# Refill instructions tied behind left operands, weight sums moved, two accumulating transfers issued later

## Chip, cores and metric

The kernel runs on one core of a Trainium2 chip. The metric is the device time of one execution in microseconds (us).

## What is computed

One layer of a bidirectional encoder with two branches, in float32, for 1024 positions, 16 meta tokens ahead of them and 1024 channels:

```python
u = rms_norm(h, pre_w)
rq, rk, rv, rg, aq, ak, av, ag, gr, ga = split(u @ w_in)
# branch A: retention, 4 heads, forward and backward scans in chunks of 128
o_r = group_norm(retention(rotary(rq), rotary(rk) * 128**-0.5, rv)) * ret_nw * silu(rg)
y_r = o_r @ w_rb
# branch B: softmax attention in a window of +-128 keys, 8 heads, meta keys, a sink logit
o_a = attention(rotary(aq), rotary(ak), av, sink) * silu(ag)
y_a = o_a @ w_ab
mix = sigmoid(gr) * y_r + sigmoid(ga) * y_a
out = h + rms_norm(mix @ w_o, post_w)
```

## The kernel before

Every large product is made three times on TensorE: an operand is split into a high part, which is its value rounded to a shorter float, and a low part, which is what the rounding left, and `mm3` multiplies high by high, low by high and high by low. So each operand costs a cast (mostly on ScalarE, `nc.scalar.copy`, sometimes on GpSimd, `pool_hi`) and a subtraction on VectorE (`dve_lo`, line 92). In the text this subtraction is "the lower part".

The work runs in this order. First come projections of the queries and keys, the retention of four heads, then attention. While attention's blocks run, projections that come later are put between them as filler. Then there are four phases of large products: z (the gate projections, 16 units), r (w_rb), a (w_ab) and o (w_out). In these four phases a product of 2x2 blocks is done with seven block products instead of eight, from sums and differences of the blocks. PROD lists the seven with their left and right operands: B11, T1, B21, T2, T3, B22 and T4 are the right operands, kept in SBUF for the whole phase, each as four pieces k = 0 to 3 in a high and a low part. They lie in the tile `big` (B11, T1, B21, B22, and T4's last piece in its margins) and in tiles named T (T2, T3, T4). A left operand belongs to one unit and one product: `prepare` builds it, from a weight tile (`wr..`) or from a sum (`st..S`), up to LEAD = 6 products ahead, and `split` makes its high part (`lh`) and its low part (`ll`); six buffers each.

`run` walks through all products in order. At each step it prepares left operands up to six products ahead, issues the product of twelve matmuls, and then calls what the dictionary `hooks` holds for this index. Two kinds of work hang there:

- The refill of the right operands for the next phase (`refill`, called for z, r and a; it is named after the phase that it runs in, so the tiles of the refill in z are named z). It loads blocks, forms differences (`minus`, line 1157), and splits them into the right operands as soon as the running phase is done with each. Indices are counted from the end of the phase: -17 is 17 products before it, 4 is after the fifth product of the next phase. The refill of phase a is another one, which gets most right operands ready-made from DRAM.
- The sums of the output weights for phase o, in four groups k = 0 to 3: `pre_load` fetches four blocks (SP), and four calls of `pre_split` each form one difference on VectorE (line 776), its high part (ScalarE) and its low part (VectorE), and write both to DRAM (SP). They are tied behind the latest sum out of PSUM (`near`).

The order in which each engine executes its instructions is not the program's. A planner simulates the kernel when it is built, with costs of its own, and fills each engine's queue with what is ready, the earlier in the program first; a later instruction can thus be put ahead of an earlier one that is not ready in the simulation. On the chip an engine works through its queue in order. `tc.issue_after(ins)` adds only an order: what is traced inside comes behind `ins` in the queue of `ins`'s engine, and instructions of other engines are not bound.

In attention, `stage1` of a block makes the scores, the exponentials, a reciprocal (`den`, line 1438) and the scaling of two weight tiles on GpSimd (line 1447), followed by two small copies on GpSimd (`pool_hi`, line 89). `stage2` transposes the scaled weights on TensorE (lines 1463 to 1468). `rope_late` turns queries and keys by their position: two products on VectorE, and two transfers issued on GpSimd that add the turned halves in place (line 187). Names of its tiles are like aq3_10: head pair 3, half 1, head 0 of the pair. `split_q` (line 669) later casts the turned queries.

Of the kernel before, what the change touches and what calls it, by code (L numbers as in the profile page):

```python
# [10 lines left out]
ALU = mybir.AluOpType  # L11
# [28 lines left out]
def block_kernel(ctx: ExitStack, tc: tile.TileContext, x0, xT, x, meta, w_in, w_rb, w_ab, w_out, post_w,  # L40
                 rope, tab, out):
    nc = tc.nc
# [48 lines left out]
    def dve_lo(o, i, hi):  # L91
        return nc.vector.tensor_tensor(o, i, hi.bitcast(F32), ALU.subtract).ins  # L92
# [84 lines left out]
    cr = ra.tile([P, T], F32, name="cr")  # L177
    sr = ra.tile([P, T], F32, name="sr")

    def rope_late(t, a, b, o, nm):  # L180

        n = b - a
        m = ra.tile([P, 512], F32, tag="m", bufs=4, name=f"m_{nm}")
        nc.vector.tensor_tensor(m[:, 0:n], t[:, 0:n], sr[:, a:b], ALU.mult)
        nc.vector.tensor_tensor(o[:, 0:n], t[:, 0:n], cr[:, a:b], ALU.mult)
        for r in (0, 64):
            nc.gpsimd.dma_start(o[64 - r:128 - r, 0:n], m[r:r + 64, 0:n], accum_op=ALU.add)

    def rope_evac(t, a, b, o, nm):
        n = b - a  # L190
# [75 lines left out]
    with tc.tile_pool(name="setup", bufs=1, reuse_waits="tile") as st:  # L266
# [87 lines left out]
        split, wv0 = halves_w(U_V)  # L354
# [409 lines left out]
    def pre_load(k, src):  # L764

        w[k] = {}
        for i, j in ((0, 0), (0, 1), (1, 1), (1, 0)):
            w[k][i, j] = t = stage(f"w{i}{j}{k}", 1)
            src(t, 4 * i + k, j)
# [12 lines left out]
        if n == "T4":  # L782
            del w[k]

    w, near = {}, []
    gates = [U_G + u for u in range(4)] + [U_AG + u for u in range(4)] + [U_GR + u for u in range(8)]

    def pre_fetch(u):
# [71 lines left out]
    softmax, last = [], {}  # L860
# [96 lines left out]
    class Phase:  # L957
# [18 lines left out]
        def split(self, u, p, src):  # L976
            h, l = (lp.tile([P, 4, P], R, tag=t, bufs=LEAD, name=f"{t}{self.nm}{u}_{p}") for t in ("lh", "ll"))
            nc.scalar.copy(h, src)
            dve_lo(l, src, h)
            self.ops[u, p] = h, l  # L980

        def prepare(self, u, p):
# [162 lines left out]
    def refill(nm, src):  # L1145

        x = {}

        def load(i, j, ks=range(4)):
            def f():  # L1150
                for k in ks:
                    x[i, j, k] = t = stage(f"{nm}{i}{j}{k}", j)
                    src(t, 4 * i + k, j)
            return f

        def minus(o, a, b):
            return lambda k: nc.vector.tensor_tensor(x[*o, k], x[*a, k], x[*b, k], sub)

        def split(n, i, j):
            return lambda k: split_b(n, k, x[i, j, k])  # L1160

        def each(at, n, *fs):
            for k in range(4):
                at.setdefault(n + k if len(fs) > 1 else n + k // 2, []).extend([lambda f=f, k=k: f(k) for f in fs])

        def got(n):
            return lambda: get_pre(n)

        def step(at, n, f):
            for k, j in enumerate(n):  # L1170
                at.setdefault(j, []).append(lambda k=k: f(k))

        if nm == "a":
            at = {-16: [load(0, 0)], -14: [load(1, 1)]}
            each(at, -13, split("B11", 0, 0))
            at.update({-11: [got("T1")], -10: [load(1, 0)], -9: [got("T2")], -5: [got("T3")], -1: [got("T4")]})
            each(at, -7, split("B21", 1, 0))
            each(at, -3, split("B22", 1, 1))
            return at

        at = {-17: [load(0, 0), load(0, 1)], -13: [load(1, 1)], -9: [load(1, 0, range(3))]}
        step(at, (-15, -14, -13, -12), minus((0, 1), (0, 1), (0, 0)))
        step(at, (-13, -12, -11, -10), split("B11", 0, 0))
        step(at, (-11, -10, -9, -8), split("T1", 0, 1))
        step(at, (-9, -8, -7, -6), minus((0, 1), (1, 1), (0, 1)))
        step(at, (-7, -6, -5, -4), split("T2", 0, 1))
        step(at, (-5, -4, -3, -2), minus((0, 0), (0, 1), (0, 0)))
        step(at, (-3, -2, -1, 3), split("B21", 1, 0))
        step(at, (-1, 0, 1, 3), minus((0, 1), (1, 0), (0, 1)))
        at[0].append(load(1, 0, (3,)))  # L1190
        step(at, (0, 1, 2, 4), split("T3", 0, 0))
        step(at, (4, 5, 6, 7), split("B22", 1, 1))
        step(at, (7, 8, 9, 10), split("T4", 0, 1))
        return at

    def run(phases):

        jobs = [(ph, u, p) for ph, _ in phases for u, p in ph.seq]
        hooks, i = {}, 0
        for ph, src in phases:  # L1200
            i += len(ph.seq)
            if src:
                for j, f in refill(ph.nm, src).items():
                    hooks.setdefault(i + j, []).extend(f)

        for u in (0, 1):
            hooks.setdefault(len(jobs) - len(ph_o.seq) - 11 + u, []).insert(0, lambda u=u: ph_o.block(u, "A11"))
        for k in range(4):
            hooks[12 * k + 16] = [lambda k=k: pre_load(k, act_src(w_out))]
            for i in range(4):  # L1210
                hooks[12 * k + 20 + 2 * i] = [lambda k=k, i=i: pre_split(k, i, near[0])]
        n = 0
        for i, (ph, u, p) in enumerate(jobs):
            while n < min(i + LEAD, len(jobs)):
                q, u_, p_ = jobs[n]
                q.prepare(u_, p_)
                n += 1
            yield
            ph.product(u, p)
            for f in hooks.get(i, ()):  # L1220
                f()
# [172 lines left out]
    def attention():  # L1394
# [14 lines left out]
        def stage1(hp, n):  # L1409
            g = hp // 2  # L1410
            kh, kl = (t.rearrange("p a b -> p (a b)") for t in kT[g])
            i = n // 4
            nm_ = ap.tile([P, 2], F32, tag="nm", bufs=3, name=f"nm{hp}_{n}")
            den = ap.tile([P, 2], F32, tag="den", bufs=3, name=f"den{hp}_{n}")
            pp = weights[n % 2]
            sides = []
            for e_ in range(2):
                if (hp, i) not in aqs or e_ not in aqs[hp, i][1]:
                    split_q(hp, e_, i)
            for x_ in range(2):  # L1420
                start, wid, seen, blocks, moff = window(n, x_)
                a_, b_ = (t[:, P * (2 * (n % 4) + x_):P * (2 * (n % 4) + x_ + 1)] for t in aqs[hp, i][0])
                s = p2(f"ps{hp}_{n}_{x_}")
                mm3(s[:, 0:wid], a_, b_, kh[:, start:start + wid], kl[:, start:start + wid], True, True)
                if n == 0 and hp:
                    raw[x_] = aw.tile([P, 337], F32, tag=f"raw{x_}", bufs=1, name=f"raw{hp}_{x_}")
                r = raw[x_]
                for c in ({0: (272, 336), 7: (208,)} if x_ else {0: (0,)}).get(n, ()):
                    nc.vector.tensor_copy(r[:, c:c + 1], nsink[:, hp:hp + 1])
                o, w0 = (0, 64) if x_ else (1, 1)  # L1430
                nc.vector.tensor_tensor_reduce(r[:, o:o + wid], s[:, 0:wid], seen, -SCALE,  # L1431
                                               nsink[:, hp:hp + 1], ALU.add, ALU.min, nm_[:, x_:x_ + 1])

                last["exp"] = nc.scalar.activation(pp[:, x_, w0 - o:w0 - o + 1 + wid], r[:, 0:1 + wid], AF.Exp,  # L1434
                                                   scale=-1.0, bias=nm_[:, x_:x_ + 1],
                                                   accum_out=den[:, x_:x_ + 1]).ins
                sides.append((wid, w0, blocks, moff))
            last["sum"] = nc.vector.reciprocal(den, den).ins  # L1438
            softmax.append(last["sum"])
            both = ap.tile([P, 2, 2, NM], F32, tag="pm2", bufs=2, name=f"pm2_{hp}_{n}")  # L1440
            ends = hp == 3 and n > 5
            for x_, (wid, w0, _, _) in enumerate(sides):
                v = pp[:, x_, w0:w0 + wid]
                if ends:
                    softmax.append(nc.scalar.activation(v, v, AF.Copy, scale=den[:, x_:x_ + 1]).ins)
                else:
                    nc.gpsimd.tensor_scalar(v, v, den[:, x_:x_ + 1], 1.0, op0=ALU.mult, op1=ALU.mult)  # L1447
            for x_, (_, w0, _, moff) in enumerate(sides):
                w_ = pp[:, x_, w0 + moff:w0 + moff + NM].unsqueeze(1).to_broadcast([P, 2, NM])
                if ends:  # L1450
                    softmax.append(nc.scalar.copy(both[:, x_], w_).ins)
                else:
                    pool_hi(both[:, x_], w_)
            pt = [lambda o, x_=x_, w0=w0: pp[:, x_, w0 + o:w0 + o + P] for x_, (_, w0, _, _) in enumerate(sides)]
            st1[hp, n] = (pt, [b for _, _, b, _ in sides], both.rearrange("p a b c -> p (a b c)"))

# [233 lines left out]
```

## Time and profile before

| what | value |
|---|---|
| median of 3 runs | 1039.8 us (1039.16 to 1040.24) |
| the profiled execution | 1040.69 us |
| its span, first to last instruction | 1038.9 us |
| busy in the span: TensorE, VectorE, ScalarE, GpSimd | 1026.2, 835.7, 502.9, 228.8 us |
| granted TensorE clock, mean | 0.996 |

A profile's times are from the start of the span. In it PE is TensorE's matmul, PEld its weight load, DVE is VectorE, ACT ScalarE, POOL GpSimd, SP the engine that issues most transfers. L92 is line 92 of the kernel before. A row of a timeline has start and duration, then engine, line, operation, output<-inputs and shapes; in brackets stands the idle time ahead of it and what ended it. A row of windows has the stretch, its length, the busy time and count of the engines that were asked for, the granted clock, the busy share of the DMA engines and GB/s.

### The profile page before, as it was taken

Reading aid. Unit: us, or ns where it says so; the run is one execution under the profiler, and the core shown is the slowest. Engines: PE = TensorE matmul, PEld = TensorE weight load, DVE = VectorE, ACT = ScalarE, POOL = GpSimd, SP = SyncE. Lnnn points to the kernel's source line nnn. Section 1 sums busy time; section 2 is a strip of 40 time slices with the busy share of each in tenths; the row PEclk is TensorE's granted clock in tenths of the full one; section 3 lists DMA queues with packets and bytes.
Section 4 is the critical chain, followed back from the end, with each engine's and each line's share of the span. In section 5 each row is a group of like instructions: output and inputs, shape, how many; then the busy total and the mean of one; then the engine's idle time right before and its main releaser. Section 6 shows DMA issues by size and latency. Waiting matters only on the chain. (4 is left out here: it accounts for less than half of the span.)

```text
span 1038.9 us, 17321 instructions
## 1 busy us (share of the span) xinstructions
PE 1026.2 (99%) x5883; PEld 900.2 (87%) x5883; DVE 835.7 (80%) x1802; ACT 502.9 (48%) x1129; POOL 228.8 (22%) x368
## 2 busy tenths in 40 slices
PE   9999999999999999999999999999999999999997
PEld 8998999989989888988888888878888788888886
DVE  7786759768876778778769998999889889778665
ACT  5531432423423466664667554456466346334442
POOL 3445244243341433444310000000000000111042
PEclk9999999999999999999999999999999999999999
DMA  9433123243241466675659688999936656789463
GB/s 360 161 87 88 63 46 85 77 85 106 80 93 62 103 177 188 178 195 157 173 173 324 216 279 296 317 350 353 365 103 205 211 171 213 228 237 319 128 122 81
DMA packets 98840, 188.45 MB, mean 181 GB/s; under 512 B 13024, under 2 KB 37632, under 8 KB 98192
## 3 DMA queue, kind: packets, MB, share of 16 engines
q1 hardware_dynamic: 81200, 162.89, 46.6%
q0 software_dynamic: 10176, 14.73, 9.6%
q10 hardware_dynamic: 7376, 9.73, 2.7%
q8 instruction: 46, 0.75, 0.3%
q14 instruction: 42, 0.34, 0.1%
HBM read 124.32 MB, written 57.68 MB: 175 GB/s over the span
## 5 line engine op out<-in xcount | busy, mean ns | idle before, releaser
L1294 POOL DMA_DIRECT2D mx_d<-c1a x4 | 3.6, 890 | 396.4 <-DVE c1a L1285 396.4
L77 PE MATMUL bz<-big,llz 128*128 128x512 f32 x192 | 74.8, 390 | 0.2 <-DVE llz L92 0.2
L78 PE MATMUL bz<-big,lhz 128*128 128x512 f32 x192 | 74.2, 389 | 0.0
L76 PE MATMUL bz<-big,lhz 128*128 128x512 f32 x192 | 73.9, 389 | 0.0
L76 PE MATMUL pv<-wh,big 128*128 128x256 f32 x256 | 72.8, 284 | 0.0
L77 PE MATMUL pv<-wh,big 128*128 128x256 f32 x256 | 72.7, 284 | 0.0
L78 PE MATMUL pv<-wl,big 128*128 128x256 f32 x256 | 72.7, 284 | 0.0
L77 PE MATMUL bz<-T,llz 128*128 128x512 f32 x176 | 68.6, 390 | 0.6 <-DVE llz L92 0.6
L78 PE MATMUL bz<-T,lhz 128*128 128x512 f32 x176 | 68.5, 389 | 0.0
L76 PE MATMUL bz<-T,lhz 128*128 128x512 f32 x176 | 68.1, 390 | 0.3 <-DVE u2z L1068 0.3
L76 PE MATMUL paq<-big,wh 128*128 128x512 f32 x128 | 51.6, 403 | 0.0
L1434 ACT ACTIVATE p<-raw,nm 128x337 f32<-128x337 f32 (+1 forms) x64 | 35.5, 556 | 32.3 <-DVE nm L1431 30.9
L77 PE MATMUL paq<-big,wl 128*128 128x512 f32 x128 | 50.3, 393 | 0.0
L78 PE MATMUL paq<-big,wh 128*128 128x512 f32 x128 | 50.2, 392 | 0.0
L1447 POOL TENSOR_SCALAR p<-p,den 128x336 f32<-128x336 f32 (+2 forms) x60 | 34.6, 623 | 66.7 <-DVE den L1438 65.2
L76 PEld LDWEIGHTS pv<-wh,big 128*128 128x128 f32 x256 | 48.4, 189 | 0.4
L77 PEld LDWEIGHTS pv<-wh,big 128*128 128x128 f32 x256 | 48.3, 189 | 0.4
L78 PEld LDWEIGHTS pv<-wl,big 128*128 128x128 f32 x256 | 48.2, 188 | 0.3
L92 DVE TENSOR_TENSOR wl<-wr,wh 128x1024 fp32r<-128x1024 f32 x28 | 35.1, 1258 | 10.5 <-POOL wh L89 6.7
L77 PEld LDWEIGHTS bz<-big,llz 128*128 128x128 f32 x192 | 36.0, 188 | 7.9 <-DVE llz L92 0.5
L78 PEld LDWEIGHTS bz<-big,lhz 128*128 128x128 f32 x192 | 36.0, 188 | 7.5
L76 PEld LDWEIGHTS bz<-big,lhz 128*128 128x128 f32 x192 | 36.0, 188 | 7.4
(621 smaller groups left out, 3599.0 us busy)
## 6 DMA issues: line engine op xcount, KB each, us to landing
wrz<-in_w_in_dram SPq DMA_DIRECT2D x32, 512.0 KB, 6.1
wr<-in_w_in_dram SPq DMA_DIRECT2D x29, 512.0 KB, 3.9
we<-in_w_in_dram SPq DMA_DIRECT2D x16, 512.0 KB, 4.3
tg<-tg_d SPq DMA_DIRECT2D x32, 256.0 KB, 5.2
e<-e ACTq DMA_DIRECT2D x20, 256.0 KB, 2.6
e<-e SPq DMA_DIRECT2D x20, 256.0 KB, 5.2
xn<-in_x_dram SPq DMA_DIRECT2D x8, 512.0 KB, 9.1
oTr_d<-ost SPq DMA_DIRECT2D x16, 256.0 KB, 2.1
```

The lines of the kernel that those rows point to most:

```text
L76: nc.tensor.matmul(o, ah, bh, start=first, stop=False, **kw)
L77: nc.tensor.matmul(o, al, bh, start=False, stop=False, **kw)
L78: latest[:] = [nc.tensor.matmul(o, ah, bl, start=False, stop=last, **kw).ins]
L92: return nc.vector.tensor_tensor(o, i, hi.bitcast(F32), ALU.subtract).ins
L1294: nc.gpsimd.dma_start(d, to, accum_op=ALU.add)
L1434: last["exp"] = nc.scalar.activation(pp[:, x_, w0 - o:w0 - o + 1 + wid], r[:, 0:1 + wid], AF.Exp, scale=-1.0, bias=nm_[:, x_:x_ + 1], accu ...
L1447: nc.gpsimd.tensor_scalar(v, v, den[:, x_:x_ + 1], 1.0, op0=ALU.mult, op1=ALU.mult)
```

## The change

Three things change. In attention the two adding transfers of aq1_10 and aq3_10 are not issued where the products are made, but after the next block's scaling and small copies on GpSimd. The four groups of output weights' sums hang at products 16, 27, 46 and 58 instead of 16, 28, 40 and 52. In the refills of z and r the first differences and the splits of T3, B22 and T4 are tied behind the lower part of the left operand that was prepared last, and in z the first loads and differences come four products earlier.

```diff
+    held = []
+    BEHIND = "aq1_10", "aq3_10"
     def rope_late(t, a, b, o, nm):
...
-        for r in (0, 64):
-            nc.gpsimd.dma_start(o[64 - r:128 - r, 0:n], m[r:r + 64, 0:n], accum_op=ALU.add)
+        def rotate():
+            for r in (0, 64):
+                nc.gpsimd.dma_start(o[64 - r:128 - r, 0:n], m[r:r + 64, 0:n], accum_op=ALU.add)
+        if nm in BEHIND:
+            held.append(rotate)
+        else:
+            rotate()
...
-    w, near = {}, []
+    w, near, ahead = {}, [], []
...
         def split(self, u, p, src):
...
-            dve_lo(l, src, h)
+            ahead[:] = [dve_lo(l, src, h)]
...
-        at = {-17: [load(0, 0), load(0, 1)], -13: [load(1, 1)], -9: [load(1, 0, range(3))]}
-        step(at, (-15, -14, -13, -12), minus((0, 1), (0, 1), (0, 0)))
+        first = -21 if nm == "z" else -17
+        at = {first: [load(0, 0), load(0, 1)], -13: [load(1, 1)], -9: [load(1, 0, range(3))]}
+        def behind(f):
+            def g(k):
+                with tc.issue_after(ahead[0]):
+                    f(k)
+            return g
+        step(at, range(first + 2, first + 6), behind(minus((0, 1), (0, 1), (0, 0))))
...
-        step(at, (0, 1, 2, 4), split("T3", 0, 0))
-        step(at, (4, 5, 6, 7), split("B22", 1, 1))
-        step(at, (7, 8, 9, 10), split("T4", 0, 1))
+        step(at, (0, 1, 2, 4), behind(split("T3", 0, 0)))
+        step(at, (4, 5, 6, 7), behind(split("B22", 1, 1)))
+        step(at, (7, 8, 9, 10), behind(split("T4", 0, 1)))
...
-        for k in range(4):
-            hooks[12 * k + 16] = [lambda k=k: pre_load(k, act_src(w_out))]
+        for k, at in enumerate((16, 27, 46, 58)):
+            hooks[at] = [lambda k=k: pre_load(k, act_src(w_out))]
             for i in range(4):
-                hooks[12 * k + 20 + 2 * i] = [lambda k=k, i=i: pre_split(k, i, near[0])]
+                hooks[at + 4 + 2 * i] = [lambda k=k, i=i: pre_split(k, i, near[0])]
...
-                    pool_hi(both[:, x_], w_)
+                    last["scaled"] = pool_hi(both[:, x_], w_)
+            if not ends:
+                with tc.issue_after(last["scaled"]):
+                    while held:
+                        held.pop(0)()
```

## The prediction

> **What bounds the kernel now.** I read the page first, then who waited for whom on TensorE, then the timelines of the engine that TensorE waited for.
>
> ```profile
> PE 1026.2 (99%) x5883; PEld 900.2 (87%) x5883; DVE 835.7 (80%) x1802; ACT 502.9 (48%) x1129; POOL 228.8 (22%) x368
> ```
>
> TensorE (PE) is busy 99% of the span: nothing but its waits, and slow matmuls after them, can be won without removing matmuls, and the change removes none. The view of waits on TensorE names them (us in total, times, longest):
>
> ```profile
> PE br L76 <- ACT lhr L978: 1.4, 1, 1.4
> PE bz L77 <- DVE llz L92: 0.8, 2, 0.6
> PE pt L1463 <- POOL p L1447: 0.7, 2, 0.5
> ```
>
> I call them the r wait, the z wait and the softmax wait. What each costs is more than its row. TensorE's timeline around the r wait (start, duration):
>
> ```profile
> 811.66 0.51 PE L76 MATMUL br<-T,lhr 128*128 128x512 f32 x1 [1.42 <-ACT lhr L978]
> ...
> 815.59 0.63 PE L77 MATMUL br<-T,llr 128*128 128x512 f32 x1
> 816.02 0.60 PE L78 MATMUL br<-T,lhr 128*128 128x512 f32 x1
> ...
> 816.69 0.40 PE L77 MATMUL br<-T,llr 128*128 128x512 f32 x1
> 816.92 0.39 PE L78 MATMUL br<-T,lhr 128*128 128x512 f32 x1
> ```
>
> Undisturbed, one such matmul starts 0.23 us after the last (816.69 to 816.92). After the wait they start 0.43 apart (815.59 to 816.02), nearly half speed. The view of windows shows the whole bill (length, busy and count of matmuls, ..., granted clock), each disturbed stretch beside an undisturbed one:
>
> ```profile
> 809.84:816.68 6.84, 5.38 (x14) 3.53 (x13) 6.54 (x11) 3.31 (x6) 0.00 (x0) 0.75 0.74 251
> 819.18:826.02 6.84, 6.84 (x32) 5.66 (x31) 5.21 (x8) 3.28 (x7) 0.00 (x0) 1.00 0.44 110
> 691.37:698.30 6.93, 6.00 (x25) 4.35 (x24) 6.93 (x13) 2.81 (x5) 0.00 (x0) 1.00 0.99 340
> 698.30:705.20 6.90, 6.90 (x32) 5.70 (x31) 6.38 (x12) 3.90 (x8) 0.00 (x0) 1.00 1.03 387
> 492.73:494.39 1.66, 0.94 (x6) 0.50 (x6) 1.63 (x3) 0.00 (x0) 1.56 (x3) 1.00 0.75 42
> 485.79:486.47 0.68, 0.68 (x9) 0.68 (x8) 0.14 (x1) 0.68 (x2) 0.00 (x0) 1.00 0.47 166
> ```
>
> An undisturbed matmul takes 6.84/30 = 0.228 us here (32 less about two that were already running at the window's start). The r stretch starts 13 (14 less one): 13 x 0.228 = 2.96 of 6.84, so 3.9 us are lost: 1.4 of waiting, 2.5 of slow and spaced matmuls at a granted clock of 0.75. The z stretch has 7 matmuls too few: 1.6 us, of which some 0.1 is the window's greater length; I take 1.5. The softmax stretch is five transposes in 1.66 us; the undisturbed one does seven in 0.68, so five in 0.49: 1.2 us lost. Together 6.6.
>
> **Part 1, ties in the refills.** Why does the r wait exist? VectorE's timeline ahead of it (0.60 from one start to the next, 810.27 to 810.87, and no idle time):
>
> ```profile
> 804.86 0.68 DVE L1157 TENSOR_TENSOR r<-r,r 128x512 f32<-128x512 f32 x1
> ...
> 810.27 0.68 DVE L1006 TENSOR_TENSOR str1S<-str1S,wrr 128x512 f32<-128x512 f32 x1
> 810.87 0.69 DVE L1157 TENSOR_TENSOR r<-r,r 128x512 f32<-128x512 f32 x1
> ```
>
> TensorE waits for a cast of a left operand made from the sum str1S, and that sum (L1006, at 810.27) stands behind three of four subtractions (L1157) of the refill for phase a, the fourth right behind it; nobody needs them for another 20 products. From 789 to 812 VectorE never rests, and this is what it does, grouped:
>
> ```profile
> L92 DVE TENSOR_TENSOR T<-z,T 128x512 fp32r<-128x512 f32 x7 | 4.6, 680 | 0.0
> L92 DVE TENSOR_TENSOR big<-z,big 128x512 fp32r<-128x512 f32 x6 | 4.0, 682 | 0.0
> L1157 DVE TENSOR_TENSOR r<-r,r 128x512 f32<-128x512 f32 x4 | 2.7, 684 | 0.0
> ```
>
> The 13 T/big rows are lower parts of right operands. One is B21's last; the others are T3, B22 and T4 (4 each). The ties put these 12 behind left lower parts of products five ahead of their hook, and the four subtractions behind those of r's products 18 to 21, so they can't come here. Not all twelve need stand ahead of the sum today; the three subtractions ahead of it alone (3 x 0.60 = 1.8 us) exceed the wait of 1.4. So the r wait goes with its slow matmuls: 3.9 us.
>
> [...]
>
> What the ties cost: they remove and add no instruction. A tied instruction blocks VectorE's queue if the left part ahead of it is not ready, and all of VectorE waits with it. The moved 12 x 0.60 = 7.2 us must fit between r's fifth and sixteenth product, where VectorE has this:
>
> ```profile
> 816.68:843.70 27.02, 21.47 (x34) 1.00 0.64 212
> 718.80:746.00 27.20, 24.34 (x41) 1.00 0.98 345
> ```
>
> 27.0 - 21.5 = 5.5 us free there (first row), 1.7 too few, but before 812 VectorE loses 16 x 0.60 = 9.6 us of work, so it enters this stretch ahead and not behind. So I cost it at nothing, with 1.7 as the bound if that cover is gone. In the z refill the first subtractions go behind the lower parts of z's products 78 to 81, and their loads start four products earlier on SP; queued behind these loads on SP are weights and gate tiles of the running phase. A load finds its buffer only when the last weight sum of part 2 has let go of it.
>
> **Part 2, output weights' sums.** Each of the four groups has eight VectorE instructions (four sums, four lower parts), twelve DMAs on SP and four casts on ScalarE. Group 1 moves one product earlier, groups 2 and 3 six later: 6 x 12 x 0.228 = 16.4 us. What the z wait waits for is seen in VectorE's timeline, and below it, from the view of one source line, all sixteen sums (first and last start):
>
> ```profile
> 676.01 0.69 DVE L776 TENSOR_TENSOR w<-w,w 128x512 f32<-128x512 f32 x1
> ...
> 692.26 0.68 DVE L92 TENSOR_TENSOR llz<-stz8S,lhz 128x512 fp32r<-128x512 f32 x1
> ...
> L776 DVE TENSOR_TENSOR w<-w,w x16: 678/682/689, 605.8 to 722.2; 128x512 f32<-128x512 f32 x16
> ```
>
> Between 676.0 and 692.3 seven of group 2's eight instructions run (four sums, three lower parts) in an unbroken queue, ahead of the left part that TensorE waits for. Moved by 16.4 us, the first comes at about 692: 7 x 0.60 = 4.2 us leave, against 1.5 lost. Gain 1.5. Group 3's last sum, at 722.2 today, comes at about 738.6. Two of its eight instructions (this sum and its lower part) lie in the stretch from 719 to 746 already, so six come into it, 3.6 us against 27.2 - 24.3 = 2.9 us of free time (second row of the windows above): 0.7 too much, a bound and not a cost, since the stretch ahead of it gets no fuller.
>
> **Part 3, the adding transfers.** The timeline of POOL, with VectorE's reciprocal that the scaling waits for ahead of it: the disturbed block, one where the scaling came 0.2 us after the transfers' issue had ended, and the block at 385:
>
> ```profile
> 489.58 0.15 DVE L1438 RECIPROCAL den<-den 128x2 f32<-128x2 f32 x1
> 490.19 1.68 POOL L187 DMA_DIRECT2D aq<-m_aq  x2 [7.32 <-ACT pah L1473]
> 491.32 2.19 POOL L1447 TENSOR_SCALAR p<-p,den 128x272 f32<-128x272 f32 x2
> 456.20 1.07 POOL L1447 TENSOR_SCALAR p<-p,den 128x336 f32<-128x336 f32 x2 [0.20 <-DVE den L1438]
> 385.28 1.66 POOL L1447 TENSOR_SCALAR p<-p,den 128x272 f32<-128x272 f32 x2
> ```
>
> The reciprocal is done at 489.73, but the scaling stands behind the two transfers' issue until 491.32, and then takes 2.19 instead of 1.07. With the transfers of aq3_10 behind it, it can run from 490.2 to 491.3, while TensorE's transposes start at 492.7 (the window above). Gain 1.2. The block at 385 (aq1_10) takes 1.66; the view of waits shows none for it, so its gain lies between 0 and 0.6, and I take 0.2. Behind the moved transfers POOL's queue holds the next block's scaling, which waits for a reciprocal of its own. The transfers are issued by about 494 instead of 491.9 (491.3, two small POOL operations, 1.68 of issue); the view of the tile gives their landing time and the timeline their reader:
>
> ```profile
> 502.69 0.62 ACT L669 CAST aqh<-aq 128x512 fp32r<-128x512 f32 x1
> DMA to landing us min/median/max: 2.7/4.1/6.5
> ```
>
> 494 + 6.5 = 500.5 against 502.7: nothing is late, and the cost is nothing.
>
> **The sum.** 3.9 + 1.5 + 1.2 + 0.2 = 6.8. Against that stands what is late next: the planner lays out all queues anew, and no row shows them. Bounds: 0.4 us more gained (other short waits go), or the 1.7 + 0.7 above come as waits. I take two waits of the z wait's size, 0.6 each: 1.3 with their edges. Net 5.5. The profiled execution took 1040.69, so 1035.2; the median of the runs is 1039.8, 0.9 lower, so 1034.3.
>
> **The rivals.**
>
> VectorE becomes the bound in phases z and r: the moved work finds no room, and waits of the bounds' size (2.4) come with one slow-clock stretch (2.5) in place of my 1.3. For it: unbroken queues from 789 to 812. Against it: the work is only spread. 1039.8 - 6.8 + 4.9 = 1037.9. Chance 0.17.
>
> The slow matmuls don't hang on the wait: TensorE's clock drops at 812 for a reason of its own, and drops again. Then 2.5 of the gain stay away, 1036.8. Against it: every other window above, also those with shorter waits, has clock 1.00, and the one drop follows the one long wait. Chance 0.04. [...]
>
> Slower: T4 becomes the wait. TensorE takes T4's products ahead of B22's today: it reads T4's last part, k = 3, from 832.11, while the left part to which that piece is now tied, of r's sixteenth product, runs at 833.42:
>
> ```profile
> 832.11 0.39 PE L76 MATMUL br<-big,lhr 128*128 128x512 f32 x1
> 833.42 0.68 DVE L92 TENSOR_TENSOR llr<-wrr,lhr 128x512 fp32r<-128x512 f32 x1
> ```
>
> If TensorE's queue keeps that order, the piece is ready at 833.42 + 0.68 + 0.60 = 834.7 at best and its third matmul wants it at 832.56: 2.1 us of waiting and 2.5 of slow clock, in phases r and a: 9.2, so 1039.8 - 6.8 + 9.2 = 1042.2. It decides wherever T4's products stand ahead of B22's. Against it: the planner knows the tie and will put B22 first, and then k = 3 is wanted two products later, at 832.56 + 24 x 0.228 = 838.0. Chance 0.11.
>
> Nothing happens: the planner's new layout puts other work of the same length where the old stood, 1039.8. Chance 0.06.
>
> **How the numbers follow.** Forecast 1034.3, chance 0.62. Its own range reaches from the whole gain and 0.4 more, 1032.6, to the first rival's 1037.9; with the second rival inside, that holds 0.83 of the chance. A measurement of this kernel tells 0.2%, 2.1 us, from no change. Faster by more: the forecast, the first rival nearly whole and the second: 0.82. Within: 0.07. Slower: 0.11.
>
> **What would show it.** Right: TensorE's view of waits without the rows of lhr, L1447 and the 0.6 of llz; granted clock 1.00 through phase r; the scaling of block (3, 0) in 1.07 us; subtractions L1157 on r tiles after 840, not at 805. Wrong: a wait of TensorE for T in phases r and a, left lower parts that end less than 1 us before their product, SP waiting for buffers between 706 and 745 with weights behind it.

## The result and the profile after

The changed kernel takes 1035.87 us (median of 6 runs, 1034.62 to 1037.15), the kernel before beside it 1039.87 (6 runs, 1039.16 to 1041.11). The ratio is 0.9957, 95% interval 0.9943 to 0.9971: 4.5 us faster by the ratio, 4.0 by the two medians. The profiled execution of the changed kernel took 1035.83 us, its span is 1034.1. The forecast was 1034.3 with a range of 1032.6 to 1037.9.

In the changed kernel's profile line numbers are 9 higher up to about line 1140, 16 higher to about 1450, and 20 higher in stage 2: the subtraction called L1157 is L1166, the scaling L1447 is L1463, the reciprocal L1438 is L1454, the left operand's cast L978 is L987, the adding transfer L187 is L192.

First the page's line on busy time, then the view of who waited for whom on TensorE (us in total, times, longest):

```profile
PE 1022.3 (99%) x5883; PEld 898.8 (87%) x5883; DVE 831.9 (80%) x1802; ACT 502.0 (49%) x1129; POOL 226.3 (22%) x368
```

```profile
PE ps L77 <- DVE aql L92: 1.0, 2, 0.5
PE ba L76 <- DVE u3a L1077: 0.6, 1, 0.6
PE pt L1483 <- DVE pal L92: 0.5, 1, 0.5
PE bz L77 <- DVE llz L92: 0.5, 1, 0.5
PE pt L1487 <- DVE pbl L92: 0.4, 1, 0.4
PE pt L1483 <- POOL p L1463: 0.2, 1, 0.2
```

The r wait (1.4) is gone, and so is the z wait at 692: the one wait for llz that is left stands at 546, where phase z begins. The softmax wait of 0.5 at 493 is gone; the 0.2 that is left of its row stands at 465, as it did before. New are short waits for u3a, pal and pbl and a second one for aql. TensorE where the r, z and softmax waits stood; the windows begin with the same matmuls as the prediction's (length, busy and count, granted clock, DMA share, GB/s):

```profile
808.29:815.13 6.84, 6.84 (x32) 1.00 0.74 225
691.33:698.26 6.93, 6.93 (x32) 1.00 1.01 368
492.73:494.39 1.66, 1.66 (x12) 1.00 0.46 139
```

All three are full, at clock 1.00. What the ties did to VectorE's queue in phase r, from its timeline, and below it the view of the source line L1166 (duration; first and last start):

```profile
805.46 0.68 DVE L92 TENSOR_TENSOR llr<-wrr,lhr 128x512 fp32r<-128x512 f32 x1
806.06 0.68 DVE L92 TENSOR_TENSOR T<-z,T 128x512 fp32r<-128x512 f32 x1
806.66 0.68 DVE L92 TENSOR_TENSOR llr<-wrr,lhr 128x512 fp32r<-128x512 f32 x1
807.26 0.68 DVE L92 TENSOR_TENSOR T<-z,T 128x512 fp32r<-128x512 f32 x1
...
829.46 0.69 DVE L92 TENSOR_TENSOR llr<-wrr,lhr 128x512 fp32r<-128x512 f32 x1
830.06 0.69 DVE L92 TENSOR_TENSOR big<-z,big 128x512 fp32r<-128x512 f32 x1
```

```profile
L1166 DVE TENSOR_TENSOR r<-r,r x16: 672/678/685, 837.1 to 869.1; 128x512 f32<-128x512 f32 x16
```

Each piece of a right operand (T, big) stands behind the left lower part (llr) to which it is tied. The twelve run from 804.9 to 830.7, where they ran between 789 and 812 before, and the subtractions for phase a start at 837.1, not at 804.9 (the prediction said after 840). VectorE in the two windows whose free time the prediction counted (length, busy and count, granted clock, DMA share, GB/s):

```profile
816.68:843.70 27.02, 24.23 (x40) 1.00 0.79 274
718.80:746.00 27.20, 24.50 (x41) 1.00 0.80 274
```

2.8 us of work came into the first (21.47 before), and room is left in both. GpSimd around the moved transfers:

```profile
490.04 0.91 POOL L1463 TENSOR_SCALAR p<-p,den 128x272 f32<-128x272 f32 x2 [7.06 <-DVE den L1454]
...
495.69 0.97 POOL L1463 TENSOR_SCALAR p<-p,den 128x272 f32<-128x272 f32 x2 [4.38 <-DVE den L1454]
...
497.21 3.36 POOL L192 DMA_DIRECT2D aq<-m_aq  x4 [0.18 <-issue]
```

The scaling runs at 490.04 in 0.91 us, where it ran at 491.32 in 2.19, begun while the second issue was still running (until 490.19 + 1.68 = 491.87). The planner put the transfers behind the scalings of two blocks, not one, so they are issued at 497.21 together with the next ones, 3.36 us for the four.

To compare whole runs, I match the 5883 matmuls of each profile with those of the first profile of the kernel before, one by one, and take how much longer or shorter each stretch between them became. Stretches are named by the first profile's times in us; negative is won. The experiments stand in it already.

| kernel (span) | to 300 | to 452 | 452-480 | 480-498 (softmax) | 498-530 | 530-640 | 640-760 (z) | 760-800 | 800-880 (r) | to the end | sum |
|---|---|---|---|---|---|---|---|---|---|---|---|
| changed (1034.1) | -0.57 | -0.27 | +0.95 | -1.32 | +0.88 | +0.29 | -1.51 | 0 | -3.90 | +0.61 | -4.84 |
| ties alone (1036.8) | -0.50 | -0.04 | +1.39 | +0.30 | -0.03 | +0.13 | 0 | 0 | -3.90 | +0.52 | -2.13 |
| sums alone (1039.1) | -0.67 | +0.27 | +1.27 | -0.03 | +0.10 | +0.16 | -1.51 | 0 | +0.61 | -0.01 | +0.19 |
| transfers alone (1039.9) | -0.37 | -0.23 | +1.26 | -1.35 | +1.28 | 0 | +0.33 | 0 | +0.04 | -0.01 | +0.95 |
| ties and sums (1034.8) | -0.45 | -0.05 | +0.31 | +0.30 | -0.03 | +0.99 | -1.51 | +0.51 | -3.90 | -0.28 | -4.12 |
| splits free (1035.2) | -0.60 | -0.20 | +0.27 | -1.35 | +1.32 | +0.18 | -1.51 | 0 | -1.85 | +0.01 | -3.73 |
| splits free, again (1036.6) | -0.48 | -0.23 | +1.16 | -1.32 | +0.83 | +0.13 | -1.51 | 0 | -0.82 | -0.02 | -2.28 |
| subtractions free (1035.9) | -0.57 | -0.23 | +1.29 | -1.32 | +1.17 | -0.02 | +0.04 | 0 | -3.90 | +0.57 | -2.98 |
| we11 sums later (1032.1) | -0.28 | -0.25 | +0.51 | -1.35 | +0.06 | -0.01 | -1.51 | 0 | -3.90 | -0.07 | -6.80 |
| copy later (1032.7) | -0.41 | -0.25 | -0.41 | -1.32 | +0.65 | +0.17 | -1.50 | +1.08 | -3.90 | -0.28 | -6.18 |
| both later (1033.8) | -0.16 | -0.23 | -0.21 | -1.32 | +0.02 | +1.89 | -1.51 | +0.56 | -3.90 | -0.28 | -5.13 |
| z's loads as before (1034.1) | -0.74 | -0.23 | +1.34 | -1.32 | +0.90 | +0.72 | -1.51 | +0.21 | -3.90 | -0.28 | -4.83 |
| before, again (1038.5) | -0.25 | -0.05 | +1.19 | -0.36 | -0.03 | +0.02 | +0.66 | 0 | -1.62 | -0.02 | -0.46 |

### The profile page after: what moved, and what is told of

Its sections match the earlier page's. It is cut to its first block, busy times and chain, and to the rows that moved or that the text cites. A ratio compares the mean times of both kernels' runs of the same rounds, so it can differ in the third digit from the quotient of the medians.

```text
span 1034.1 us, 17322 instructions
## 1 busy us (share of the span) xinstructions
PE 1022.3 (99%) x5883; PEld 898.8 (87%) x5883; DVE 831.9 (80%) x1802; ACT 502.0 (49%) x1129; POOL 226.3 (22%) x368
## 5 line engine op out<-in xcount | busy, mean ns | idle before, releaser
L1463 POOL TENSOR_SCALAR p<-p,den 128x336 f32<-128x336 f32 (+2 forms) x60 | 32.6, 565 | 85.9 <-DVE den L1454 81.1
```

## The experiments

**Each part alone, and the first two together.** Each kernel is the changed one without some of these edits:

```diff
 # A, without part 3
-    BEHIND = "aq1_10", "aq3_10"
+    BEHIND = ()
 # B, without part 2
-        for k, at in enumerate((16, 27, 46, 58)):
+        for k, at in enumerate((16, 28, 40, 52)):
 # C, without part 1 (B22 and T4 like T3)
-        first = -21 if nm == "z" else -17
+        first = -17
-        step(at, range(first + 2, first + 6), behind(minus((0, 1), (0, 1), (0, 0))))
+        step(at, range(first + 2, first + 6), minus((0, 1), (0, 1), (0, 0)))
-        step(at, (0, 1, 2, 4), behind(split("T3", 0, 0)))
+        step(at, (0, 1, 2, 4), split("T3", 0, 0))
```

Ties alone is A and B, sums alone A and C, transfers alone B and C, ties and sums A.

> Only part 1: the ties in the refills and z's earlier loads; sums and transfers as before. Theory (each wait is paid where it stands): the r wait and its slow matmuls go, 3.9 us, the z wait of 1.5 stays: 1036.0 plus up to 0.7 us of new waits in phase a, so 1035.9 to 1036.7. Rival (the clock drops at 812 for a reason of its own): only the 1.4 us of waiting go, the matmuls 0.43 apart stay: 1038.4. Rival (T4 becomes the wait): slower than 1039.9, with a wait of TensorE for T in phase r.

> Only part 2: the output weights' sums at 16, 27, 46, 58. Theory: the z wait goes, the r wait stays with its slow matmuls: 1039.9 - 1.5 = 1038.4. Rival (VectorE's queue is only full elsewhere): no change, 1039.9, with a wait between 715 and 745.

> Only part 3: the adding transfers of aq1_10 and aq3_10 behind a scaling. Theory (attention is paced by transfers that land when they land, so TensorE's 1.4 us come back as waits before phase z begins): 1039.9 within 0.4, with the matmul of phase z that waits for llz at about 546.4 as before. Rival (a gain of 1.2 to 1.4 that another run's late landing at 457 hid): 1038.6.

> The changed kernel without part 3. Theory (part 3 is worth nothing in time): as the changed kernel, 1035.9 within 0.4. Rival (part 3 is worth 1.2 to 1.4): 1037.2.

Measured, as ratio to the kernel before on the same chip (1040.73 us, 29 runs, 1038.88 to 1043.65): ties alone 0.9968, interval 0.9955 to 0.998 (1038.18 us); sums alone 0.9999, 0.999 to 1.0008 (1040.82); transfers alone 0.9993, 0.9984 to 1.0003 (1040.02); ties and sums 0.9958, 0.9945 to 0.9971 (1036.48). TensorE's waits with the ties alone, with the sums alone and with the transfers alone:

```profile
PE bz L77 <- DVE llz L92: 1.0, 2, 0.7
```

```profile
PE br L76 <- ACT lhr L987: 1.9, 1, 1.9
```

```profile
PE br L76 <- ACT lhr L987: 1.4, 1, 1.4
PE bz L77 <- DVE llz L92: 1.1, 2, 1.0
PE ps L77 <- DVE aql L92: 1.1, 2, 0.6
```

The ties alone take away the r wait and leave the z wait. The sums alone take away the z wait, but the r wait grows from 1.4 to 1.9: won 1.51 at z, lost 0.61 at r, and no gain in the time, where 1038.4 was expected. The transfers alone take away the softmax wait (1.35) and lose 1.28 in the next stretch, in a second wait for aql. Parts 1 and 2 together have the whole gain of the change; part 3 is worth nothing that these runs can tell from zero. The time of the ties alone missed its expectation too, by 1.5 us.

Both misses go with the granted clock, whose mean is on record for every run. In the first profile the granted clock is 0.50 for 3.41 us behind the r wait, from 813.04 to 816.45; one such stretch takes 3.41 x 0.50 / 1039 = 0.0016 off the mean. The three profiles with such a stretch in phase r (the first, the sums alone, the transfers alone) have 0.996, the eleven others 0.998 or 0.999. Of the kernel before, 16 of 61 runs beside the experiments have 0.996 or 0.997, and their medians are 1.6 to 2.0 us above those of the others. Of the sums alone it is ten of twelve, of the transfers alone four of twelve, of the ties alone none, of the ties and sums none of six, and of the changed kernel none of six. By this reading the half clock is a price that the kernel before paid in about one run of four, and with the sums alone in most: it hides their gain, and the 3.9 expected of the ties holds 1.6 that most runs beside them never paid. That these runs had the half clock in phase r is read from the means; no trace of them was kept.

**Which half of the ties takes the r wait away?** One kernel has the splits of T3, B22 and T4 free and the subtractions tied; the other the reverse.

```diff
 # splits free (B22 and T4 like T3)
-        step(at, (0, 1, 2, 4), behind(split("T3", 0, 0)))
+        step(at, (0, 1, 2, 4), split("T3", 0, 0))
...
 # subtractions free
-        step(at, range(first + 2, first + 6), behind(minus((0, 1), (0, 1), (0, 0))))
+        step(at, range(first + 2, first + 6), minus((0, 1), (0, 1), (0, 0)))
```

> The changed kernel with the splits of T3, B22 and T4 free again; the four subtractions of each refill stay tied, parts 2 and 3 stay. Theory (the prediction's step): the three subtractions ahead of the sum, 3 x 0.60 = 1.8 us, are what TensorE waited for, so taking them away is enough: no r wait, or a rest of at most 0.3 us (1.9 us was the r wait in the run with part 2 alone, 0.1 more than 1.8), granted clock 1.00 from 809 to 817, and the changed kernel's time, ratio to before 0.995 to 0.997 (1034.7 to 1036.8). Rival: the twelve lower parts of T3, B22 and T4, 7.2 us, are the burden, and the wait stays at 1 us or more with a granted clock of about 0.75, 3.5 to 4.5 us lost there, ratio 0.999 to 1.001.

> The changed kernel with the first subtractions of both refills free again (z's still four products earlier); the splits of T3, B22 and T4 stay tied, parts 2 and 3 stay. Theory: there is more work ahead of the sum than the wait is long, so this half is enough as well: twelve lower parts, 7.2 us, leave the stretch from 789 to 812, the subtractions stand ahead of the sum again, and still no r wait; ratio 0.995 to 0.997, as for the other half. Rival: the subtractions alone make the wait, since VectorE's queue gives them the place wherever they are free; r wait of 1 us or more, ratio 0.999 to 1.001.

Splits free: 0.9987, 0.9974 to 1.0 (12 runs, 1036.95 to 1042.34, median 1039.14). Subtractions free: 0.9984, 0.9973 to 0.9995 (12 runs, 1034.75 to 1041.5, median 1039.44). Neither interval reaches the changed kernel's ratio. TensorE's waits, splits free, and then subtractions free:

```profile
PE br L77 <- DVE llr L92: 1.4, 2, 1.2
```

```profile
PE bz L76 <- DVE u2z L1077: 1.2, 1, 1.2
```

With the splits free an r wait stays, although no subtraction for phase a stands ahead of it any more: from 785 to 810 VectorE's queue has no gap, and the twelve lower parts of T3, B22 and T4 are in it. With the splits tied and the subtractions free this profile has no r wait. But a wait of 1.2 us comes up at 750, and VectorE's timeline shows from where:

```profile
748.50 1.29 DVE L1166 TENSOR_TENSOR z<-z,z 128x512 f32<-128x512 f32 x2 [3.49 <-DMA tg_d<-c5z]
749.71 0.68 DVE L1077 TENSOR_TENSOR u2z<-e,bz 128x512 f32<-128x512 f32 x1
```

Two free subtractions of the refill in z stand 3.49 us at the head of VectorE's queue, for a transfer; behind them stands the sum out of PSUM (u2z) that TensorE waits for, the 1.2 us above. (The row names a transfer that stores c5z; what the two subtractions read is loaded, so I take the end of a load for the cause, which the trace doesn't show.) In the changed kernel the tie keeps that sum ahead of them (it runs at 745.94). So the splits' ties clear the way to the left operands of r, and the subtractions' ties keep an instruction that has to wait for a transfer from blocking VectorE. The second need may come from the change itself: this kernel keeps z's start four products earlier, and in the profiles with free subtractions and the old start (before twice, sums alone, transfers alone) no wait stands at 750. A kernel with the splits tied, the subtractions free and the old start wasn't run, so that both halves are needed without the earlier start is not shown. How much the blocking costs is open too: the profile is 1.9 us behind the changed kernel's, the ratio 2.8, and five of the twelve runs have a granted clock of 0.996 or 0.997, whose slow stretch no trace shows.

**The same kernel again**, since its profiled run was the fastest of twelve:

> The same kernel as e5_minus_tied, looked at a second time: its twelve runs went from 1036.95 to 1042.34 and the profiled one was the lowest of them, with an r wait of 1.16 us at a granted clock of 1.00 (2.0 us lost there), while waits of 1.4 to 1.9 us in other kernels came with 0.75 to 0.85 and 3.9 to 4.5 us lost. Theory: the split halves leave a wait that lies at the point where the clock drops, so other runs of it pay the 2 to 2.5 us of slow matmuls too; this run, if it is at 1038.5 or more, shows granted clock below 0.9 between 805 and 815 and 3.5 us or more lost there. Rival: the spread comes from waits elsewhere (landing times in attention, phase z); then the clock at 805 to 815 is 1.00 again, about 2.0 us lost, and the difference stands before 790.

```profile
PE br L77 <- DVE llr L92: 2.4, 2, 1.3
```

This run took 1038.41 us. The granted clock stayed at 1.00 from 805 to 815, and none of the twelve runs with free splits has a mean below 0.998, so the theory falls: not the clock, but longer waits made it slower, 1.03 us in r and 0.89 in 452-480, where the table has the two runs in neighbouring rows.

**Are the loads of z four products earlier of use?**

```diff
-        first = -21 if nm == "z" else -17
+        first = -17
```

> The changed kernel with the first loads and subtractions of the refill in z back at 17 products ahead of the end (they stay tied). Theory: what counts is that the subtractions and splits stand behind left operands; the four products' earlier start gives only room for them. The subtractions end later by 4 x 12 x 0.228 = 11 us, and B21's and T2's splits with them, so at the end of z VectorE is fuller: waits of 0 to 0.6 us at 790 to 812, ratio 0.995 to 0.997. Rival: the earlier start is what makes it work; without it the splits meet the left operands of r again, an r wait of 1 us or more, with 2 to 4.5 us lost, ratio 0.998 to 1.001.

0.9953, 0.9939 to 0.9967 (1036.25 us): the changed kernel's time within the interval, and no r wait. What the ties do doesn't rest on the earlier start.

**Where the gain in attention goes.** In the changed kernel TensorE waits 0.53 us for the lower part of a query at 516.85. VectorE's timeline:

```profile
504.51 0.69 DVE L813 TENSOR_TENSOR we<-we,we 128x512 f32<-128x512 f32 x1 [1.31 <-DMA we<-in_w_in_dram]
505.12 0.68 DVE L92 TENSOR_TENSOR aql<-aq,aqh 128x512 fp32r<-128x512 f32 x1
```

A weight sum on we waits for its load, and the query's lower part aql, with everything behind it, waits with it. With ties and sums only VectorE's row ahead of it (pm) starts 0.48 us later (503.10 for 502.62), and still this load's sum starts at 504.42, 0.09 earlier: the landing didn't come earlier with the rest. The experiment hangs the three sums one filler product later:

```diff
-164: [(split_q, 3, 0, 1)], 166: [(pre_sum, 11, 0)], 167: [(pre_sum, 11, 1)], 168: [(pre_sum, 11, 2)],
+164: [(split_q, 3, 0, 1)], 167: [(pre_sum, 11, 0)], 168: [(pre_sum, 11, 1)], 169: [(pre_sum, 11, 2)],
```

> The changed kernel with the three sums of the projection weights we11 hung one filler product later (167, 168, 169 for 166, 167, 168); nothing else moves on the queues but these sums, behind the lower part of aq3_10's query. Theory: the 0.5 us wait for aql at 516.85 (0.66 us with what is around it) comes from a sum on we at 504.51 that waits for its load to land and holds VectorE's queue, the lower part of the query behind it. It goes: no aql wait there, 0.7 us won in the profile between 499 and 519, and nothing new later; ratio to before 0.994 to 0.996. Rival: the query is late by itself, because aq3_10's transfers were issued only at 497.21; then the wait stays at 0.4 to 0.6 us, and time is the changed kernel's.

```profile
503.07 0.69 DVE L92 TENSOR_TENSOR aql<-aq,aqh 128x512 fp32r<-128x512 f32 x1
...
508.28 1.41 DVE L813 TENSOR_TENSOR we<-we,we 128x512 f32<-128x512 f32 x2
```

aql runs at 503.07 and no longer stands behind the load; the 0.88 us lost in 498-530 is 0.06. 1034.05 us (5 runs, 1033.85 to 1034.65), ratio 0.9942, 0.9931 to 0.9954. With the sums there, part 3's gain is kept.

**The wait at 457.** It comes in nearly all profiles, in different lengths. ScalarE's timeline in the changed kernel, and below it in one where a 1 MB copy in DRAM comes six blocks later:

```profile
451.99 0.41 ACT L724 CAST kTh<-akr 128x256 fp32r<-128x256 f32 x1 [1.69 <-DMA akr<-m_ak]
```

```diff
-            if k in (12, 14, 21):
-                x_to_out({12: 0, 14: 4, 21: 6}[k])
+            if k in (12, 20, 21):
+                x_to_out({12: 0, 20: 4, 21: 6}[k])
```

> The changed kernel with one 1 MB copy from x to out, which SP issued at 441.95, put six blocks later (about 482). Theory: this copy is what delays the landing of akr's adding transfers, issued at 443.60 and read by the cast at 451.99; without it the cast starts by 450, and the 0.5 us wait at 457.30 (0.64 to 1.05 us over the runs so far) goes: 0.6 us won between 452 and 466, if the copy doesn't harm its new place. Rival: the transfers take 8 us by themselves there; cast at 451.5 to 452.3 and the wait stays at 0.4 to 0.7 us.

```profile
449.03 0.41 ACT L724 CAST kTh<-akr 128x256 fp32r<-128x256 f32 x1
```

The cast waits for nothing and starts at 449.03, 5.3 us after its transfers' issue began (443.78) instead of 8.4 (443.60 to 451.99). In the twelve profiles with the copy in its old place the cast starts 7.2 to 8.9 us after the issue began and always waits for the transfers; in the two with the copy moved it starts 5.3 and 5.5 us after it and waits for nothing. The stretch 452-480 is 1.36 us shorter than in the changed kernel, and 0.4 to 1.8 shorter than in all kernels with the copy in its old place. 1034.32 us (6 runs), 0.9947, 0.9935 to 0.996. In its profile another wait of 0.8 us, for llz, stands at 789; its cause stays open.

**Both mendings together:**

> The changed kernel with both mendings: the we11 sums one filler product later (as in e7_sums_later) and the 1 MB copy six blocks later (as in e8_copy_later). Theory: their gains are at different places (499 to 518, 452 to 466) and add: e7 and e8 stood at ratios 0.9942 and 0.9947, the changed kernel at 0.9957, so 0.992 to 0.994, 1032 to 1034 us where before is at 1040; no wait of TensorE at 457 nor for aql at 515. Rival: the copy in its new place delays the we load or the xs loads, a new wait of 0.5 us or more appears between 480 and 520, and the time is that of the better of the two, ratio 0.994 to 0.995.

1034.28 us (5 runs, 1032.41 to 1035.55), ratio 0.9932, 0.9919 to 0.9946. Both stretches are as short as expected, and still it can't be told from the kernel with the sums moved alone. Its profiled run, the slowest of the five, has a wait of another place; TensorE's timeline:

```profile
636.85 0.50 PE L76 MATMUL bz<-T,lhz 128*128 128x512 f32 x1 [1.27 <-ACT u2z L1074]
```

The three mended kernels have ratios below the changed kernel's 0.9957. Their intervals all meet its own (0.9943 to 0.9971), that of both mendings only just, and each other; among the three no best one can be named.

**The kernel before again:**

> The kernel before, looked at a second time, because its runs go from 1038.4 to 1043.8 and its one profile lacks the wait at 457 that nearly all other profiles have. Theory: r wait of 1.4 us or more with a granted clock of 0.75 to 0.85 in 810 to 820 again, z wait of 1 to 1.8 us, softmax wait at 493; a wait of 0.4 to 1.1 us at 457 to 458, which belongs to no part of the change. Rival: no wait at 457, so that it is the changed order of the queues that brings it.

1040.23 us. TensorE's waits, and its window around the r wait:

```profile
PE bz L77 <- DVE llz L92: 1.5, 2, 1.3
PE br L76 <- ACT lhr L978: 1.4, 1, 1.4
...
PE pt L1463 <- DVE pal L92: 0.6, 1, 0.6
PE pt L1463 <- POOL p L1447: 0.6, 2, 0.3
```

```profile
811.02:817.86 6.84, 5.40 (x22) 1.00 0.76 261
```

The waits of the expectation are there, the one at 457 too (1.19 us more in 452-480 than in the first profile), so it belongs to no part of the change. But the clock is 1.00: the r wait of 1.4 us is the same as in the first profile, and 22 matmuls lie in the window where 14 did, ten too few instead of eighteen. 10 x 0.228 = 2.3 us are lost there, 1.4 of waiting and 0.9 of matmuls that start 0.4 to 0.5 apart right behind the wait at full clock. So of the first profile's 2.5 us of slow and spaced matmuls only some 1.6 are the clock's, and they are not there in every run.

## Why the prediction came out right, step by step

**The r wait (3.9).** It is gone, with clock 1.00, and the table has 3.90. The reason given for it was wrong. The prediction said that the three subtractions ahead of the sum alone, 1.8 us, exceed the wait of 1.4 and so decide. With these tied and the splits free, r waits of 1.4 and 2.4 us in total stayed. Taking three instructions out of a queue that is laid out anew doesn't make it 1.8 us shorter at that place: the planner fills the room. It is the twelve lower parts that had to go; once they were tied, the planner put no subtraction for phase a there, tied or not. The change tied both halves, so the time came out; with only the half that the prediction held for sufficient it was 0.9987 of the kernel before. In this the right time was luck. And of the 3.9, some 1.6 is a matter of the run, since the kernel before pays it in one profile and not in the other (3.90 less 1.62 is 2.3). By the mean granted clocks (0.996 or 0.997 in 16 of 61 runs) about one run of four pays it.

**The slow clock (the second rival, 0.04).** The rival said that the slow matmuls don't hang on the wait. It is half borne out: up to the last matmul the half clock comes in these profiles behind three long waits, but not behind others nearly as long, and its price is some 1.6 us, not 2.5. The granted clock fell to 0.5 behind waits of 1.42 (first profile), 1.43 (transfers alone) and 1.91 us (sums alone). It stayed at 1.00 behind 1.40 and 1.32 (before, again, at 812 and 693), and the profiles with waits of 1.27 (both later) and 1.24 (subtractions free) have means of 0.998 and 0.999, without room for such a stretch. In the first profile the matmuls start 0.43 apart from 813.04 to 816.44, for 3.4 us, at a granted clock of 0.50, and 0.23 apart from 816.69 on. With the sums alone and the transfers alone the windows of 2 us from 812 to 818 (clock 0.82, 0.50, 0.83 and 1.00, 0.51, 0.64) make up 3.4 us at 0.5 as well.

Around the waits of 1.42 and 1.40 us TensorE's timelines hardly differ: behind the first the next matmul starts 0.52 us after the one that had waited (811.66, 812.18), behind the second 0.53 (812.82, 813.35), and then the one profile goes on at half clock and the other at full. Why the clock fell in the one and not in the other these runs don't show, nor how long a wait it takes.

**The z wait (1.5).** Right: 1.51. The runs with the sums alone add what the prediction didn't see: without the ties the r wait grows from 1.4 to 1.9, and the part alone is worth nothing in the time (ratio 0.9999).

**The softmax wait (1.2, and 0.2 at 385).** Both right at their place: 1.32, and 0.27 between 300 and 452, where the other kernels with the moved transfers have about the same (0.20 to 0.25) and those without have from 0.05 won to 0.27 lost. As terms of the sum they failed, because the prediction costed the transfers' delay only for the tile that they bring ("nothing is late"), and not for what waits for other things next. That tile was indeed not late, though the transfers were issued at 497.21 and not by 494. Late was the load of a weight, which didn't come earlier with the rest (its sum starts at 504.51 here and at 504.42 with ties and sums only); 0.88 of the 1.32 were paid there, 20 us further on, and the sums moved one place later show it.

**What is late next (1.3).** In the profile it was 0.95 + 0.88 + 0.29 + 0.61 = 2.73, less 0.57 won ahead of 300 us. The 7.0 won at the four waits less 2.16 are the 4.84 of the span. The size was a guess; the 0.95 is no cost of the change, since the second profile of the kernel before has 1.19 there. Nor is the 0.57 a gain of it, since all other profiles won 0.16 to 0.74 there, the kernel before too. With the 1.62 of the clock, 0.57 + 1.62 - 0.95 = 1.24 of the 4.84 belong to the first profile and not to the change: 3.6 are left, near the 4.0 of the medians and well under the forecast's 5.5. That the time fell into the range all the same it owes to the range's width. The 0.61 near 942 comes in three kernels with the splits tied and not in others; its cause stays open.

**VectorE as the bound (first rival, 0.17).** Phase r has no waits of that size. VectorE had room for the moved work (24.23 us busy of 27.02, and 24.50 of 27.20), and the bounds of 1.7 and 0.7 cost nothing.

**T4 becomes the wait (0.11).** TensorE's waits name no T in phases r and a. T4's last piece was ready at 830.06 + 0.69 = 830.75, not at 834.7.

**Nothing happens (0.06).** The interval of the ratio excludes it for the change. With the splits free it came near: there the planner filled the room, as this rival had it.

**What stays open.** Why the runs of one kernel differ: those of the kernel with free splits go over 5.4 us, those with the we11 sums moved over 0.8. The pairs of profiles show that single waits differ by 0.4 to 1.2 us between runs, among them those at 457 behind a transfer (1.19 and 0.89 in 452-480), but the profiles are too few to say which of them makes the spread.

## What to carry to other kernels

A wait that is taken away is kept as a gain only if what comes next doesn't hang on a transfer with a landing time of its own: of the 1.32 us won at the softmax wait 0.88 were lost again behind one, and 0.06 once the sums on its load hung later. So look at the 20 us behind it, at the head of each engine's queue, for instructions whose idle time ends with a DMA, and move those back. Work that is free to go early is not free: on VectorE here it delayed what stood behind it by its own length, 0.60 us for each subtraction, and where its data landed late by that too (1.31 us at 504.51 in the changed kernel, 3.49 at 748.50 with the subtractions free). Before a stretch's cost is put into a sum, look at it in a second profile: here two fifths of the greatest term were there in one profile of the kernel before and not in the other. And compare the mean granted clock of all runs, not of the profiled one alone.

## What the hardware showed that was not expected

Behind a wait of TensorE of 1.42 us in one profile of the kernel before the granted clock fell to 0.50 for 3.41 us, which cost some 1.6 us; behind one of 1.40 us in the other it stayed at 1.00. What told the two apart is not shown. Two adding transfers of 64x256 floats had landed within 5.5 us of the start of their issue without a 1 MB DRAM copy just ahead of them, and were waited for until 7.2 to 8.9 us after it with one. The scaling on GpSimd took 2.19 us behind the issue of two transfers and 0.91 ahead of them.
